# A transformer block in one launch, first gemm of its FFN: accumulating transfers that read the weights from HBM, a second quarter split by VectorE, a fourth quarter loaded once, and wide matmuls grouped by width

## The chip, the core and the metric

The kernel runs on one core of a Trainium2 chip. The metric is the device time of one execution in microseconds (us). Engines: TensorE (PE; PEld for its weight loads), VectorE (DVE), ScalarE (ACT), GpSimd (POOL, which here mostly issues transfers) and SyncE (SP, which issues the weight loads). PSUM is where matmuls leave their sums, SBUF where all other tiles lie, HBM the memory outside the core. Each engine works through its own list of instructions in order; an instruction that waits holds back all that stand behind it on that engine.

## The reference, cut to what matters

One block on 512 tokens of width 1024, all in fp32: a mixer with two attention branches, then a gated FFN, with a modulation by a condition vector. The change touches the FFN's first gemm alone (`w_ffn_in`, 1024 x 5632):

```python
h2 = modulate(rmsnorm(x, g_norm2[l]), shift2, scale2)
a, u = split(einsum('bsd,de->bse', h2, w_ffn_in[l]), 2)   # 2816 columns each
x = x + gate2[:, None, :] * einsum('bse,ed->bsd', silu(a) * u, w_ffn_out[l])
```

## The kernel before, in words

**Hi and lo.** TensorE multiplies in a rounded fp32 form, so every operand is split in two tiles: a rounded `hi`, and `lo`, which holds what the rounding lost. A product takes three matmuls: hi with hi, hi with lo and lo with hi. `high` (L846) makes hi by a ScalarE copy (L847). lo is made in one of two ways. `low` (L850) subtracts on VectorE, raw minus hi (L851). `low_dma` (L838) lets ScalarE write minus hi (L839) and then lets a transfer, issued by GpSimd, add the raw weight to it on the way (L840): an accumulating transfer, which reads the raw tile in SBUF. `split_dma` is `high` and then `low_dma`. The weights of the FFN's second gemm are split by ScalarE (L206) and VectorE (L208) after a load by L201.

**Blocks and products.** The 2816 columns of a and of u are cut into 11 blocks p = 0 to 10, 256 columns of a and 256 of u each. The weight of a block is a 2 x 2 of quarters (row half, column half), each 128 x 1024 elements or 512 KB: quarter (1,0) is called the second here and (1,1) the fourth. Instead of eight quarter products a block does seven, in the manner of Strassen and Winograd, with sums of quarters as weights:

```python
SUM = {5: ((0, 1), (0, 0)), 6: ((1, 1), 5), 4: ((1, 0), 6), 7: ((1, 1), (0, 1))}
```

So t5 = (0,1) - (0,0), t6 = (1,1) - t5, t4 = (1,0) - t6 and t7 = (1,1) - (0,1), on VectorE (L1222). Product 1 takes quarter (0,0), 2 takes (1,0), 3 takes (1,1), and 4 to 7 take t4 to t7. The activations' sums stand in SBUF as pairs, ah next to al (`v`, `qp`, `q`, `z` and so on by `act7`).

**Where weights come from.** `load_ff` (L1199) lets SyncE load a quarter. (0,0) and (1,0) go to a `raw` tile, of which there are 3 and which the second gemm's weights share; (0,1) and (1,1) go to an `araw` tile, of which there are 2. The fourth quarter is loaded twice in a block: into `araw` for the sums t6 and t7, and again into `raw` for product 3 (L1231). Products 1 and 2 get their lo by an accumulating transfer, product 3 and the sums by VectorE. `prepare` (L1225) does a weight's load, hi and lo; `prepare_item` (L1238) does it with the sums that are due.

**Two ways to multiply.** Blocks 0 and 1 use `product` (L1258), with matmuls 256 columns wide. Blocks from 2 on use `wide_product` (L1286): hi goes against ah and al side by side, 512 columns, and lo against ah, 256 columns, over 4 steps of the contraction into each of two PSUM banks: 16 matmuls in a product. `both_sums` (L1295) takes the two halves of a bank out, ScalarE by a copy (L1299) and VectorE by an add (L1300); `both_added` (L1303) does it by VectorE alone (L1308). Products 1, 6, 7 and 4 of a block go one after another into the same two banks, so 6 must be taken out before 7 starts.

**Order.** A list of work (L1418) puts a block's products as 1, 5, an item of the second gemm (`out`), 6, 2, 7, 3, 4, another `out`. Weights are prepared five items ahead (L1414). The first part, on products of blocks 0 and 1 and on the weights of block 2's products 1 and 2, is written out by hand (L1464 to L1598). Elsewhere a scheduler puts each engine's list in order; it is the tile framework's, and gives a load its place once the tile that it overwrites is due to be free.

Of the kernel before, what the change touches and what calls it, by code (L numbers as in the profile page):

```python
# [12 lines left out]
F32R = mybir.dt.float32r  # L13
I32 = mybir.dt.int32
AF = mybir.ActivationFunctionType
ALU = mybir.AluOpType
# [5 lines left out]
S = 512  # L22
# [70 lines left out]
WIDX = {e[0]: n for n, e in enumerate(PLAN)}  # L93
# [22 lines left out]
def kernel(  # L116
# [9 lines left out]
    nc = tc.nc  # L126
# [9 lines left out]
    def nm(s):  # L136
        uid[0] += 1
        return f"{s}_{uid[0]}"

    def ps():  # L140
        return pspool.tile([P, S], F32, tag="ps", bufs=BUFS["ps"], name=nm("ps"))
# [4 lines left out]
    def psz():  # L146
        return pspool.tile([P, S], F32, tag="z", bufs=BUFS["z"], name=nm("z"))
# [4 lines left out]
    def tmp():  # L152
        return apool.tile([P, S], F32, tag="t", bufs=BUFS["t"], name=nm("t"))
# [7 lines left out]
    def f(ap):  # L161
        return ap.bitcast(F32)
# [64 lines left out]
    def mm(o, lhs, rhs, start, stop):  # L227
        return nc.tensor.matmul(o, lhs, rhs, start=start, stop=stop, skip_group_check=True).ins  # L228
# [211 lines left out]
    with tc.manual_schedule(engines={nc.vector.engine, nc.scalar.engine, nc.tensor.engine}):  # L440

        nc.scalar.preload_act_table_set("natural_log_exp_and_others")
        c = sm[:, SM_C : SM_C + KT]
# [36 lines left out]
        for hv in HALVES:  # L480
            o = psz()[:, 0:256]
# [28 lines left out]
        for kt in range(KT):  # L510
# [8 lines left out]
            raw, hi, lo = wts[kt]  # L519
            ah, al = hs[kt][:, 0, :], hs[kt][:, 1, :]  # L520
# [303 lines left out]
    def quarter(tag):  # L824
        return pair(tag).rearrange("p a b -> p (a b)")

    def tiles(t):
        return t.rearrange("p (k c) -> p k c", k=4)

    def raw_quarter(tag):  # L830
        return apool.tile([P, 2 * S], F32, tag=tag, bufs=BUFS[tag], name=nm(tag))

    def wtile(tag):
        if tag in ("s", "h", "q", "v"):
            return quarter(tag)
        return wpool.tile([P, WCOLS], F32R, tag=tag, bufs=BUFS[tag], name=nm(tag))

    def low_dma(src, hi, lo):  # L838
        nc.scalar.activation(lo, f(hi), AF.Copy, scale=-1.0)  # L839
        nc.gpsimd.dma_start(f(lo), src, accum_op=ALU.add)  # L840
        return hi, lo

    def split_dma(src, hi, lo):
        return low_dma(src, high(src, hi), lo)

    def high(t, hi):  # L846
        nc.scalar.activation(hi, t, AF.Copy)  # L847
        return hi

    def low(t, hi, lo):  # L850
        nc.vector.tensor_sub(lo, t, f(hi))  # L851
        return hi, lo
# [242 lines left out]
    for h in range(17):  # L1095
        heads(h)
        p = h // 2 + 2
# [13 lines left out]
    for d in range(8):  # L1111
        o = ps()
        gemm(o, weight(("ps", d)), acts)
        r, t = tmp(), tmp()
# [60 lines left out]
    def high7(key, src, tags):  # L1175
        acts7[key] = two = [quarter(t) for t in tags]
        for n, t in enumerate(two):
            ins = nc.scalar.activation(
                parted(t)[:, :, 0, :], src[:, n * S : n * S + S].rearrange("p (k c) -> p k c", k=2), AF.Copy
            )  # L1180
        return ins.ins
# [9 lines left out]
    def act7(key, k):  # L1191
        t = acts7[key][k // 2]
        c = k % 2 * S
        return t[:, c : c + 256], t[:, c + 256 : c + S], t[:, c : c + S]

    ready = {}
    raws_of, sums_of = {}, {}

    def load_ff(p, half, c, tag):  # L1199
        if tag in ("h", "q"):  # L1200
            r = raw_quarter(tag)
            nc.sync.dma_start(r, wp[WIDX["ff", p, half, c]])
            return r
        r = wpool.tile([P, WCOLS], F32, tag=tag, bufs=BUFS[tag], name=nm(tag))
        nc.sync.dma_start(r, wp[WIDX["ff", p, half, c]])
        return r
# [3 lines left out]
    def load_raws(p, quarters):  # L1210
        raw = raws_of.setdefault(p, {})
        for q in quarters:
            if q not in raw:
                raw[q] = load_ff(p, *q, "araw" if q[1] else "raw")

    def sums(p, **tags):
        raw, t = raws_of[p], sums_of.setdefault(p, {})
        for key, tag in tags.items():
            n = int(key[1])
            a, b = SUM[n]  # L1220
            t[n] = raw_quarter(tag)
            ins = nc.vector.tensor_sub(t[n], raw[a], t[b] if b in t else raw[b])  # L1222
        return ins.ins

    def prepare(p, n, tags=None):  # L1225

        if n < 3:
            load_raws(p, [(n - 1, 0)])
            w = split_dma(raws_of[p][n - 1, 0], *(wtile(t) for t in tags or " sh"[n] * 2))
        elif n == 3:  # L1230
            raw = load_ff(p, 1, 1, "raw")  # L1231
            w = low(raw, high(raw, wtile("whi")), wtile("wlo"))
        else:
            t = sums_of[p][n]
            w = low(t, high(t, wtile("whi")), wtile("wlo"))
        ready[p, n] = w

    def prepare_item(it):  # L1238
# [3 lines left out]
        p, n = it  # L1242
        if p > 1 and n == (5 if p >= WIDE else 6):
            sums(p, t5="s", t6="s")
# [10 lines left out]
    SEVEN = {1: "A11", 2: "A12", 3: "S4", 4: "A22", 5: "S1", 6: "S2", 7: "S3"}  # L1255
# [30 lines left out]
    def wide_product(p, n, banks, first, last):  # L1286
        hi, lo = (tiles(t) for t in ready.pop((p, n)))
        for i, o in enumerate(banks):
            c = slice(i * P, (i + 1) * P)
            for k in range(4):  # L1290
                ah, _, both = act7(SEVEN[n], k)
                mm(o, hi[:, k, c], both, first and k == 0, False)
                mm(o[:, 256:S], lo[:, k, c], ah, False, last and k == 3)

    def both_sums(banks, t=None):  # L1295
        t = t or tmp()
# [14 lines left out]
    def run_wide(p, n):  # L1311
# [6 lines left out]
        elif n == 2:  # L1318
            d["y"] = [psz(), psz()]
        banks = d["v" if n in (3, 5) else "y" if n == 2 else "z"]  # L1320
        wide_product(p, n, banks, n in (1, 5, 2) or alone and n == 6, n in (2, 3, 4))
        added = (lambda b: both_added(d["p1"], b, tmp())) if alone else both_sums
        if n == 1:
# [20 lines left out]
    def store_act(p, *halves):  # L1344
# [3 lines left out]
            split(hi[:, :, hv], lo[:, :, hv], t.rearrange("p (a b) -> p a b", a=2))  # L1348
        ff_acts[chunk_of[p]] += [(hi[:, i, :], lo[:, i, :]) for i in range(2)]
        del part[p]  # L1350

    WIDE = 2

    def run_product(p, n):

        if p >= WIDE:
            return run_wide(p, n)
# [62 lines left out]
    for c, (p0, n) in enumerate(FF_CHUNKS):  # L1420
        for p in range(p0, p0 + n):
            wide = p >= 2
            for n_, m in enumerate((1, 6, 5, 2, 7, 3, 4) if p == 1 == WIDE else (1, 5, 6, 2, 7, 3, 4) if wide else (1, 6, 5, 7, 2, 4, 3)):
                if (p, m) not in FIRST:
# [13 lines left out]
    for d in range(4):  # L1438
        o = ps()
# [24 lines left out]
    with tc.manual_schedule(engines={nc.vector.engine, nc.scalar.engine, nc.tensor.engine}):  # L1464
# [55 lines left out]
        first = load_ff(1, 1, 0, "raw")  # L1520
        raws_of[1][1, 0] = first
        b_hi = high(first, wtile("whi"))
# [2 lines left out]
        )  # L1525
        d0["p1"] = tmp()
        nc.scalar.activation(d0["p1"], d0["x"], AF.Copy)
        ready[1, 2] = low_dma(first, b_hi, wtile("wlo"))
        k5 = high(t0[5], wtile("whi"))
        r1 = []  # L1530
        product(0, 2, d0["x2"], True, True, 4, lambda: r1.append(half_bcast(g1)))
# [10 lines left out]
        k1 = high(raws_of[2][0, 0], wtile("s"))  # L1542
# [12 lines left out]
        d0["z"], d0["v"], d0["w"] = psz(), psz(), psz()  # L1555
        product(0, 6, d0["z"], True, True, late="a")
        high7("S1", s1, ("qp", "q"))
        ready[2, 1] = low_dma(raws_of[2][0, 0], k1, wtile("s"))
        nc.vector.tensor_sub(s3, m00, s3)
        low7("S1", s1)  # L1560
        high7("S3", s3, "qq")
# [2 lines left out]
        d0["u2"] = tmp()  # L1564
        nc.vector.tensor_add(d0["u2"], d0["z"], d0["p1"])
        b22 = load_ff(0, 1, 1, "raw")
        ready[0, 3] = split_dma(b22, wtile("whi"), wtile("wlo"))
        high7("S4", s4, "qq")
        prepare(2, 2)
        load_raws(1, [(0, 1), (1, 1)])  # L1570
# [57 lines left out]
    for d in FULL:  # L1628
        o = ps()
# [158 lines left out]
```

## Time and profile before

| what | value |
|---|---|
| time, 3 runs | 1129.54 us median, 1128.47 to 1130.91 |
| time of the profiled execution | 1134.42 us |
| its span, first to last instruction | 1132.7 us |
| mean granted TensorE clock | 0.991 of full |
| VectorE, ScalarE, GpSimd busy | 868.0, 571.7, 49.9 us |
| HBM read, written | 146.35 MB, 16.78 MB |
| blocks 4 to 10 of the FFN's first gemm | 873 us to about 1100 us of the span |

A chain of waits lists start, length and what ran. A timeline row is start, length, engine, line, operation, tiles and shape; the bracket gives how long its engine had idled before it and what released it. A row of windows gives the window's ends and length, busy time (with instructions) of PE, PEld, DVE, ACT and POOL, then the granted clock, the share of the DMA engines' time, and GB/s. A row of waits is: who waited, for what, us in total, times, longest.

### The profile page before, as it was taken

The page shows a single profiled execution, that of the slowest core. Times are in us where ns is not written, and L with a number is a line of the kernel's source. Part 1 is how long each engine was busy: PE and PEld are TensorE (multiplying, and loading weights), DVE is VectorE, ACT ScalarE, POOL GpSimd, SP SyncE. Part 2 cuts the span into 40 slices and gives each one's busy share as a digit, 9 for nine tenths or more (in the row PEclk, how much of TensorE's full clock was granted, in tenths as well). Part 3 has the DMA queues.
Part 4 walks back from the last instruction along what each step waited for, and adds up shares of the span by engine and source line. Part 5 has one row for each costly group of instructions (what it writes and reads, how often), then busy time and mean ns, then how long its engine had stood idle before and what let it go on. Part 6 is the DMA issues. An engine that isn't in the chain of part 4 may idle for free.

```text
span 1132.7 us, 15139 instructions
## 1 busy us (share of the span) xinstructions
PE 1109.7 (98%) x5607; PEld 938.8 (83%) x5607; DVE 868.0 (77%) x1306; ACT 571.7 (50%) x935; POOL 49.9 (4%) x78
## 2 busy tenths in 40 slices
PE   8999999999999999999999999999999999999996
PEld 6888888887788888888888888899988788877886
DVE  7889856958977958387778757668999778868766
ACT  5445345434444645355656553449555545545543
POOL 0000000010020020000000000000000000000000
PEclk9999999999999999999999999999999999998998
DMA  9724432765775476866676569453547635555312
GB/s 353 284 71 149 140 120 81 221 134 196 240 166 196 157 156 231 220 195 186 182 205 160 161 194 320 157 146 81 165 128 193 201 96 161 168 149 152 90 56 76
DMA packets 63146, 190.86 MB, mean 169 GB/s; under 512 B 7776, under 2 KB 9824, under 8 KB 63072
## 3 DMA queue, kind: packets, MB, share of 16 engines
q1 hardware_dynamic: 55760, 171.02, 46.7%
q0 software_dynamic: 6768, 18.35, 9.5%
q8 instruction: 44, 0.72, 0.3%
q10 hardware_dynamic: 544, 0.52, 0.1%
q14 instruction: 30, 0.25, 0.1%
HBM read 146.35 MB, written 16.78 MB: 144 GB/s over the span
## 4 chain that ended last, share of the span: by engine, by line
PE 79%; DVE 10%; DMA 6%; issue 3%; ACT 2%; SPq 0%; DVEq 0%; ACTq 0%; POOLq 0%
PE ps L228 60%; PE z L228 11%; PE av L228 6%; DMA araw<-wada 2%; DMA raw<-wp 2%; DVE araw L256 1%; DVE wlo L851 1%; PE ps L636 1%; DVE s L870 1%; DVE wlo L208 1%; DMA s<-raw 1%; DMA sraw<-wada 1%; DVE t L758 0%; PE z L762 0%; DMA h<-raw 0%
## 5 line engine op out<-in xcount | busy, mean ns | idle before, releaser
L228 PE MATMUL ps<-h,whi 128*128 128x512 f32 (+1 forms) x1026 | 294.8, 372 | 0.0
L228 PEld LDWEIGHTS ps<-h,whi 128*128 128x128 f32 x1026 | 185.3, 189 | 32.1 <-ACT sm L410 0.2
L206 ACT ACTIVATE whi<-raw 128x1024 fp32r<-128x1024 f32 (+1 forms) x104 | 108.6, 1045 | 203.7 <-PE ps L228 160.4
L228 PE MATMUL ps<-h,wlo 128*128 128x512 f32 (+1 forms) x513 | 188.1, 370 | 0.0
L208 DVE TENSOR_TENSOR wlo<-raw,whi 128x1024 fp32r<-128x1024 f32 (+1 forms) x104 | 125.0, 1202 | 74.9 <-ACT whi L206 74.4
L228 PE MATMUL ps<-q,whi 128*128 128x512 f32 (+1 forms) x368 | 131.1, 402 | 5.8 <-DVE t L1300 5.7
L228 PEld LDWEIGHTS ps<-h,wlo 128*128 128x128 f32 x513 | 96.7, 188 | 16.6
L228 PE MATMUL ps<-s,whi 128*128 128x512 f32 x320 | 98.9, 390 | 0.3 <-DVE s L208 0.3
L228 PE MATMUL ps<-q,wlo 128*128 128x256 f32 (+1 forms) x328 | 97.4, 297 | 0.0
L228 PEld LDWEIGHTS ps<-q,whi 128*128 128x128 f32 x368 | 70.5, 193 | 24.3 <-DVE t L1300 8.1
L851 DVE TENSOR_TENSOR wlo<-s,whi 128x1024 fp32r<-128x1024 f32 x46 | 56.1, 1222 | 44.2 <-ACT whi L847 44.1
L847 ACT ACTIVATE whi<-s 128x1024 fp32r<-128x1024 f32 x47 | 49.6, 1058 | 51.4 <-PE ps L228 42.4
L228 PE MATMUL ps<-whi,h 128*128 128x512 f32 x222 | 71.6, 391 | 0.0
L228 PEld LDWEIGHTS ps<-s,whi 128*128 128x128 f32 x320 | 60.1, 188 | 13.2 <-DVE s L208 0.6
L228 PEld LDWEIGHTS ps<-q,wlo 128*128 128x128 f32 x328 | 63.9, 195 | 1.3
L228 PE MATMUL ps<-s,wlo 128*128 128x512 f32 x160 | 62.2, 389 | 0.0
L228 PEld LDWEIGHTS ps<-whi,h 128*128 128x128 f32 x222 | 41.7, 188 | 9.5 <-ACT t L991 0.6
L847 ACT ACTIVATE whi<-raw 128x1024 fp32r<-128x1024 f32 x28 | 29.7, 1059 | 34.1 <-PE ps L228 32.6
L256 DVE SCALAR_TENSOR_TENSOR araw<-araw,cact 128x1024 f32<-128x1024 f32 x32 | 39.1, 1228 | 8.4 <-DMA araw<-wada 8.3
L851 DVE TENSOR_TENSOR wlo<-raw,whi 128x1024 fp32r<-128x1024 f32 x26 | 31.8, 1223 | 16.7 <-ACT whi L847 16.7
L228 PE MATMUL ps<-wlo,h 128*128 128x512 f32 x111 | 43.2, 390 | 0.0
L1299 ACT ACTIVATE t<-ps 128x256 f32<-128x256 f32 x82 | 30.1, 372 | 23.1 <-PE ps L228 23.0
(349 smaller groups left out, 2242.5 us busy)
## 6 DMA issues: line engine op xcount, KB each, us to landing
raw<-wp SPq DMA_DIRECT2D x145, 512.0 KB, 4.0
araw<-wada SPq DMA_DIRECT2D x32, 512.0 KB, 4.0
araw<-wp SPq DMA_DIRECT2D x30, 512.0 KB, 4.6
s<-wp SPq DMA_DIRECT2D x24, 512.0 KB, 5.9
sraw<-wada SPq DMA_DIRECT2D x16, 512.0 KB, 8.0
q<-qp SPq DMA_DIRECT2D x32, 256.0 KB, 4.5
spill<-o POOLq DMA_DIRECT2D x24, 256.0 KB, 4.9
o<-xT SPq DMA_DIRECT2D x16, 256.0 KB, 4.4
```

What stands on the lines that cost most here:

```text
L206: nc.scalar.activation(dst_hi, src, AF.Copy, scale=scale)
L208: return (eng or nc.vector).tensor_sub(dst_lo, src, f(dst_hi))
L228: return nc.tensor.matmul(o, lhs, rhs, start=start, stop=stop, skip_group_check=True).ins
L256: nc.vector.scalar_tensor_tensor(raw, raw, 1.0, cact, op0=ALU.mult, op1=ALU.mult, accum_out=col)
L636: nc.tensor.transpose(at[bank][:, c : c + P], t[:, a + j * P : a + (j + 1) * P], ident)
L847: nc.scalar.activation(hi, t, AF.Copy)
L851: nc.vector.tensor_sub(lo, t, f(hi))
L870: nc.vector.tensor_tensor(dst[:, d], *((y, x) if swap else (x, y)), op=op)
L1299: nc.scalar.activation(c, o[:, 0:256], AF.Copy)
```

## The change

Four edits, all in the first gemm of the FFN:

- `low_dma`'s transfer takes the raw weight from HBM, where it was loaded from, not from the raw tile in SBUF. The raw tile is then read by the hi copy and the sums alone.
- For blocks from 2 on the second quarter's lo is made by `low` on VectorE, with no copy of minus hi and no transfer. In the part written by hand this is `prepare(2, 2)`.
- For blocks from 2 on product 3 uses the fourth quarter as it lies in `araw`; its second load is gone, and the `araw` tile is now read by t6, t7, and product 3's hi and lo.
- `wide_product` does the four 512-column matmuls of a bank first, and then its four 256-column ones.

```diff
     def low_dma(src, hi, lo):
         nc.scalar.activation(lo, f(hi), AF.Copy, scale=-1.0)
-        nc.gpsimd.dma_start(f(lo), src, accum_op=ALU.add)
+        nc.gpsimd.dma_start(lo, src.bitcast(F32R), accum_op=ALU.add)
...
+    WIDE, LOWD = 2, (2,)
...
         if n < 3:
             load_raws(p, [(n - 1, 0)])
-            w = split_dma(raws_of[p][n - 1, 0], *(wtile(t) for t in tags or " sh"[n] * 2))
+            hi, lo = (wtile(t) for t in tags or " sh"[n] * 2)
+            raw = raws_of[p][n - 1, 0]
+            w = (low(raw, high(raw, hi), lo) if p >= WIDE and n in LOWD else
+                 low_dma(wp[WIDX["ff", p, n - 1, 0]], high(raw, hi), lo))
         elif n == 3:
-            raw = load_ff(p, 1, 1, "raw")
+            raw = raws_of[p][1, 1] if p >= WIDE else load_ff(p, 1, 1, "raw")
             w = low(raw, high(raw, wtile("whi")), wtile("wlo"))
...
             for k in range(4):
-                ah, _, both = act7(SEVEN[n], k)
-                mm(o, hi[:, k, c], both, first and k == 0, False)
-                mm(o[:, 256:S], lo[:, k, c], ah, False, last and k == 3)
+                mm(o, hi[:, k, c], act7(SEVEN[n], k)[2], first and k == 0, False)
+            for k in range(4):
+                mm(o[:, 256:S], lo[:, k, c], act7(SEVEN[n], k)[0], False, last and k == 3)
...
-        ready[1, 2] = low_dma(first, b_hi, wtile("wlo"))
+        ready[1, 2] = low_dma(wp[WIDX["ff", 1, 1, 0]], b_hi, wtile("wlo"))
...
-        ready[2, 1] = low_dma(raws_of[2][0, 0], k1, wtile("s"))
+        ready[2, 1] = low_dma(wp[WIDX["ff", 2, 0, 0]], k1, wtile("s"))
...
-        ready[0, 3] = split_dma(b22, wtile("whi"), wtile("wlo"))
+        ready[0, 3] = low_dma(wp[WIDX["ff", 0, 1, 1]], high(b22, wtile("whi")), wtile("wlo"))
```

Lines of helpers move by one to four: L1299, L1300 and L1308 become L1303, L1304 and L1312, L1222 becomes L1223, L1205 becomes L1206.

TensorE's list before, at the start of product 1 of block 4 (`ps_7994` is the product's first PSUM bank, `v` the pair ah and al, `s_7829` the weight's hi and `s_7830` its lo):

```order
L228 MATMUL ps_7994<-v_6764,s_7829 128x512
L228 MATMUL ps_7994<-v_6764,s_7830 128x256
L228 MATMUL ps_7994<-v_6764,s_7829 128x512
L228 MATMUL ps_7994<-v_6764,s_7830 128x256
L228 MATMUL ps_7994<-v_6765,s_7829 128x512
L228 MATMUL ps_7994<-v_6765,s_7830 128x256
```

The same product after the change (`ps_7987` is its bank, `s_7823` hi and `s_7824` lo):

```order
L228 MATMUL ps_7987<-v_6764,s_7823 128x512 x2
L228 MATMUL ps_7987<-v_6765,s_7823 128x512 x2
L228 MATMUL ps_7987<-v_6764,s_7824 128x256 x2
L228 MATMUL ps_7987<-v_6765,s_7824 128x256 x2
```

The wide and the narrow matmuls of a bank no longer take turns; their number is the same.

VectorE's list before, in block 6 from the lo of its product 3 on (`raw_8573` is the fourth quarter's second load; `araw_8668`, `raw_8661` and `araw_8670` are block 7's (0,1), (0,0) and (1,1); the first L1222 is block 7's t5 and the second its t6; L1158 adds a result to the residual):

```order
L851 TENSOR_TENSOR wlo_8577<-raw_8573,whi_8575 128x1024
L1300 TENSOR_TENSOR t_8597<-t_8597,ps_8580 128x256
L1158 SCALAR_TENSOR_TENSOR o_6349<-z_8606,mod,o_6349 128x512
L1222 TENSOR_TENSOR s_8695<-araw_8668,raw_8661 128x1024
L1222 TENSOR_TENSOR s_8697<-araw_8670,s_8695 128x1024
L1158 SCALAR_TENSOR_TENSOR o_6351<-av_8620,mod,o_6351 128x512
L851 TENSOR_TENSOR wlo_8604<-h_8514,whi_8602 128x1024
L1300 TENSOR_TENSOR t_8656<-t_8656,ps_8550 128x256
L208 TENSOR_TENSOR wlo_8637<-raw_8634,whi_8636 128x1024
L1300 TENSOR_TENSOR t_8656<-t_8656,ps_8551 128x256
```

The same place after (`araw_8380` is block 6's fourth quarter, `araw_8655` block 7's, `t_8641` takes product 6 of block 6 out of its banks):

```order
L851 TENSOR_TENSOR wlo_8562<-araw_8380,whi_8560 128x1024
L1304 TENSOR_TENSOR t_8582<-t_8582,ps_8565 128x256
L1223 TENSOR_TENSOR s_8680<-araw_8653,raw_8646 128x1024
L1158 SCALAR_TENSOR_TENSOR o_6349<-z_8591,mod,o_6349 128x512
L1223 TENSOR_TENSOR s_8682<-araw_8655,s_8680 128x1024
L851 TENSOR_TENSOR wlo_8589<-h_8501,whi_8587 128x1024
L1158 SCALAR_TENSOR_TENSOR o_6351<-av_8605,mod,o_6351 128x512
L1304 TENSOR_TENSOR t_8641<-t_8641,ps_8537 128x256
L208 TENSOR_TENSOR wlo_8622<-raw_8619,whi_8621 128x1024
L1304 TENSOR_TENSOR t_8641<-t_8641,ps_8538 128x256
```

The order is nearly the same, but product 3's lo now reads the `araw` tile that block 7's fourth quarter will overwrite. In some blocks (7 is one) product 2's lo, a new L851, stands between the last two L1304.

SyncE's list before, from block 6's second load of its fourth quarter on:

```order
L1205 DMA raw_8573<-wp 128x1024
L201 DMA raw_8634<-wp 128x1024
L1205 DMA araw_8668<-wp 128x1024
L1205 DMA raw_8661<-wp 128x1024
L1205 DMA araw_8670<-wp 128x1024
L201 DMA raw_8725<-wp 128x1024
L1205 DMA raw_8785<-wp 128x1024
L1205 DMA raw_8851<-wp 128x1024
```

The same place after (`raw_8495` is block 6's second quarter):

```order
L1206 DMA raw_8495<-wp 128x1024
L201 DMA raw_8619<-wp 128x1024
L1206 DMA raw_8646<-wp 128x1024
L201 DMA raw_8710<-wp 128x1024
L1206 DMA araw_8653<-wp 128x1024
L1206 DMA araw_8655<-wp 128x1024
L1206 DMA raw_8770<-wp 128x1024
```

The loads `raw_8573` and `raw_8851` have no counterpart, and the two `araw` loads of block 7 stand behind one more load of the second gemm.

More of the change, by code (lines that the diff above doesn't have):

```diff
@@ L1350, in store_act @@
         del part[p]
-    WIDE = 2
     def run_product(p, n):
```

## The prediction

> **What bounds the kernel now.** I read the page first, for the engine that bounds; then the chain of waits, for the places where that engine's rhythm breaks; then the windows and the timeline there, and SyncE's waits. The page:
>
> ```profile
> span 1132.7 us, 15139 instructions
> ...
> PE 1109.7 (98%) x5607; PEld 938.8 (83%) x5607; DVE 868.0 (77%) x1306; ACT 571.7 (50%) x935; POOL 49.9 (4%) x78
> ```
>
> TensorE is busy for 98% of the span. So only three things count: matmul work, TensorE's few idle times, and its clock. In the chain the first product of a block shows as one piece of 32 matmuls. These are the starts of blocks 4, 5, 6, 9 and 10:
>
> ```profile
> 873.05 5.64 PE ps L228 x32
> 907.88 5.64 PE ps L228 x32
> 938.57 5.64 PE ps L228 x32
> 1037.88 5.64 PE ps L228 x32
> 1068.57 5.64 PE ps L228 x32
> ```
>
> Undisturbed, a block takes 938.57 - 907.88 = 30.69 us, as does 1068.57 - 1037.88. Block 4 took 34.83, so 4.14 too many. Blocks 6 to 8 took 99.31, against 3 x 30.69 = 92.07: 7.24 too many. Together 11.4 us. The windows on those two places, and on one undisturbed block:
>
> ```profile
> 873.00:904.00 31.00, 28.77 (x145) 24.13 (x144) 23.81 (x37) 15.41 (x23) 1.72 (x2) 0.94 0.63 176
> 1000.00:1038.00 38.00, 34.98 (x167) 29.13 (x166) 25.58 (x40) 17.92 (x27) 1.72 (x2) 0.91 0.53 152
> 1038.00:1068.60 30.60, 30.60 (x161) 26.10 (x160) 24.18 (x38) 15.09 (x24) 1.72 (x2) 1.00 0.33 87
> ```
>
> TensorE idles 31.00 - 28.77 = 2.2 us in the first and 3.0 in the second, and the clock costs 0.06 x 31 = 1.9 and 0.09 x 38 = 3.4: 4.1 and 6.4 of the 4.14 and 7.24. The first two rows below are the chain at the second place, the others its timeline:
>
> ```profile
> 1006.95 6.22 DMA s<-raw
> 1013.73 4.34 DMA raw<-wp
> ```
> ```profile
> 1013.31 0.33 SPq L201 DMA_DIRECT2D raw<-wp  x1
> 1018.18 1.06 ACT L847 ACTIVATE h<-raw 128x1024 fp32r<-128x1024 f32 x1 [5.22 <-DMA raw<-wp]
> 1019.54 0.42 DVE L1300 TENSOR_TENSOR t<-t,ps 128x256 f32<-128x256 f32 x1 [4.11 <-ACT t L1299]
> 1020.01 0.50 PE L228 MATMUL ps<-q,whi 128*128 128x512 f32 x1 [2.29 <-DVE t L1300]
> 1021.47 0.63 PE L228 MATMUL ps<-q,whi 128*128 128x512 f32 x1
> ```
>
> Read it downwards. An accumulating transfer lands at 1013.17, and until then holds the raw tile that it reads. Only then can SyncE issue the load of 1013.31, with the second quarter's load behind it at 1013.73. ScalarE, in order, has stood for 5.22 us at that quarter's hi; the PSUM copy L1299 stands behind it, VectorE's L1300 waits for the copy, and TensorE waits 2.29 us for the bank. Afterwards a wide matmul takes 0.63 us. At the first place the same chain; the first row is from SyncE's waits between 884 and 892 us:
>
> ```profile
> SPq L1205 <- DMA s<-raw: 6.4, 1, 6.4
> ```
> ```profile
> 894.23 1.06 ACT L847 ACTIVATE h<-raw 128x1024 fp32r<-128x1024 f32 x1 [6.01 <-DMA raw<-wp]
> 897.67 0.61 PE L228 MATMUL ps<-q,whi 128*128 128x512 f32 x1 [2.23 <-DVE t L1300]
> ```
>
> **The change, part by part.** *Transfers from HBM, second quarter on VectorE.* SyncE's waits for accumulating transfers between 840 and 1100 us:
>
> ```profile
> SPq L201 <- DMA s<-raw: 37.0, 3, 12.7
> SPq L1205 <- DMA s<-raw: 26.9, 4, 7.1
> SPq L201 <- DMA h<-raw: 22.2, 4, 9.2
> SPq L1205 <- DMA h<-raw: 11.0, 4, 7.2
> ```
>
> These 97 us go, because no transfer reads a raw tile any more. A raw tile is then free once ScalarE and VectorE have read it, and block 4's load, which came behind a wait of 6.4 us, could have been issued up to 6.4 us sooner. TensorE stood for 2.2 and 2.3 us, so both stalls vanish whole, and the lowered clock with them: **-11.4 us**. What is late next is the `araw` load, below. Bounds: 0, if the load is as late for another reason, and -11.4.
>
> Nine copies of minus hi and nine transfers go; nine subtractions come:
>
> ```profile
> L851 DVE TENSOR_TENSOR wlo<-raw,whi 128x1024 fp32r<-128x1024 f32 x26 | 31.8, 1223 | 16.7 <-ACT whi L847 16.7
> ```
>
> ScalarE, at half load, gets nine copies free: 0. By this row VectorE gets 9 x 1.22 more, one in a block: 24.18 + 1.22 = 25.4 of 30.7 us, 83%. TensorE hides it, unless it falls ahead of a PSUM add that TensorE waits for; that is priced below.
>
> The transfers that remain read the same 512 KB from HBM. The page of accumulating issues (min, median, max to landing) beside the plain loads:
>
> ```profile
> DMA to landing us min/median/max: 4.5/4.8/8.9
> ```
> ```profile
> raw<-wp SPq DMA_DIRECT2D x40, 512.0 KB, 3.6
> araw<-wp SPq DMA_DIRECT2D x14, 512.0 KB, 5.2
> ```
>
> Product 1's weight is issued a block ahead: a transfer from 1006.95 serves block 9, from 1037.88. That is 31 us of cover, and only a landing over 31 us would cost. I take 0.
>
> *Fourth quarter loaded once.* Nine loads of 512 KB go. In exchange block p+1's fourth quarter can't be loaded before block p's product 3 has its lo, and VectorE's t6 waits for it in order. Behind t6 stand t4's lo, a residual add, the lo of `out`, and the L1300 that takes product 6 out, which product 7 needs. Block 6's VectorE before:
>
> ```profile
> 945.22 1.23 DVE L851 TENSOR_TENSOR wlo<-raw,whi 128x1024 fp32r<-128x1024 f32 x1 [1.55 <-ACT whi L847]
> 948.91 1.23 DVE L1222 TENSOR_TENSOR s<-araw,s 128x1024 f32<-128x1024 f32 x1
> 950.05 0.74 DVE L1158 SCALAR_TENSOR_TENSOR o<-av,mod,o 128x512 f32<-128x512 f32 x1
> 953.50 1.23 DVE L208 TENSOR_TENSOR wlo<-raw,whi 128x1024 fp32r<-128x1024 f32 x1 [1.24 <-ACT whi L206]
> 954.64 0.41 DVE L1300 TENSOR_TENSOR t<-t,ps 128x256 f32<-128x256 f32 x1
> ```
> ```profile
> 949.67 2.71 PE ps L228 x15
> ```
>
> That lo ends at 946.45. The load lands 3.6 (raw's median) to 5.2 us (araw's) later: 950.1 to 951.7. With a residual add ahead of it t6 could start at 948.6, so VectorE waits 1.5 to 3.1 us. Then follow t6 1.2, t4's lo 1.2, residual 0.7, add 0.4, lo of `out` 1.2 and add 0.4, less 0.1 of overlap each: about 4.9 us, until 955.0 to 956.6. Product 6 ends at 952.38, product 2 takes 2.83, so product 7 starts at 955.2 and reaches its second bank 1.4 later, at 956.6. The wait is 0. In the blocks where product 2's lo stands in between too (+1.14), it is 0 to 1.1 us. For seven blocks that is 0 to 7.7 us; I take **+1.8**, nearer to 0, since VectorE had 30.60 - 24.18 = 6.4 us of slack in a block.
>
> *Opening.* `prepare(2, 2)` now puts a subtraction into VectorE's list, ahead of block 2's t5, in a stretch where one row follows on the other without a pause. The lo that is needed soonest after it:
>
> ```profile
> 802.68 1.22 DVE L851 TENSOR_TENSOR wlo<-s,whi 128x1024 fp32r<-128x1024 f32 x1
> ```
>
> What follows is 1.2 us later, and up to 1.1 more (one hi copy, as L847 above) if its hi isn't ready. The lo of 802.68 is used a few us later. 0 to +2.3, I take **+0.5**: TensorE's next products have weights ready.
>
> *Wide matmuls grouped.* The chain has pieces of one width each and mixed ones:
>
> ```profile
> 913.52 2.74 PE z L228 x12
> 797.07 2.88 PE z L228 x24
> 918.98 2.81 PE ps L228 x16
> 921.79 2.83 PE z L228 x16
> ```
>
> Twelve wide ones: 2.74/12 = 0.2283 us each. Twenty-four narrow ones: 0.120 each. A grouped product is 8 x 0.2283 + 8 x 0.120 = 2.786 against 2.81 to 2.83: 0.024 to 0.044 less. Block 2 has 5 wide products left, 8 blocks have 7: 61 x 0.034 = **-2.1** (-1.5 to -2.7; 0 if a change of width costs nothing).
>
> A weight load takes 0.195 us by the next row, longer than a narrow matmul's 0.120:
>
> ```profile
> L228 PEld LDWEIGHTS ps<-q,wlo 128*128 128x128 f32 x328 | 63.9, 195 | 1.3
> ```
>
> So a load runs beside matmuls of its own rows. The Trainium skill, TensorE: Matmul & The Clock Gate, section "The mechanism", has it that a weight load overlaps matmuls in flight only where row groups differ; here all use all rows, so load and matmul would add up in any order and this term would be 0. The trace disagrees: 0.120 us is less than the 0.195 of one load.
>
> **Sum.** 1134.4 - 11.4 - 2.1 + 0.5 + 1.8 = 1123.2 us for an execution like the profiled one. That one lies 4.9 over the median of the runs. If the 4.9 belongs to profiling, the timed runs fall to 1118.3; if the timed runs merely had less of those stalls, they land at 1123.2. I take the middle, **1121.0**.
>
> **Rivals.** *The gain is eaten, or was never there.* Either the second quarter's load stays late for another reason, or the `araw` wait takes 5 to 8 us. With grouping alone: 1129.5 - 2.1 = 1127.4; with grouping and VectorE's other costs 1127 to 1131. For it: SyncE's list is in order, and the `araw` load now stands in it waiting for VectorE, ahead of the next second quarter. Against it: both stalls lead back to an accumulating transfer by name. Chance 0.16.
>
> *Slower: the fourth quarter holds TensorE up in every block.* Place: t6, behind an `araw` load that lands over 6.5 us after its issue, where 5.2 is the median. VectorE then runs 2.3 us or more late at product 6's add, TensorE idles as at 897.67, and each stall costs what block 4's did, 4.14 us with its clock. From the third on, the 8.5 us forecast are gone; with five of seven blocks 1121 + 5 x 4.1 = 1141.5, with eight 1154. For it: two loads issued together shared the DMA engines. Against it: a block's DMA share is 0.33 where nothing is late, and eleven loads and transfers become nine or ten. Chance 0.13.
>
> Here a rule would change the price. In the trace, 2.23 us of idling were followed by matmuls of 0.61 to 0.63 us and a window clock of 0.94. The Trainium skill, TensorE: Matmul & The Clock Gate, section "HAM oscillation — how this bites in real kernels", lets the clock fall for idle gaps over about 3.4 us; by it five stalls of 2.3 us would cost 11.5 and end near 1132.5, still slower. The trace disagrees: 2.2 us was enough.
>
> *The forecast* has the rest, 0.71, own range 1115 to 1126.
>
> **How the numbers follow.** The forecast's range takes the unknown terms at both ends: 1118.3 less 2.3 for a late wait that never comes and 0.6 for grouping gives 1115; 1123.2 with 2.5 more of waits gives 1126. To hold 8 in 10 it reaches into the first rival, up to 1129, and one down, 1114. About 0.2% (2.3 us) is what a measurement of this kernel can tell from no change. Faster by more, under 1127.2: the forecast and a little of the first rival, 0.73. Within: 0.13, the rest of that rival. Slower, above 1131.8: 0.14, the second rival and a sliver of the first.
>
> **What would show it.** Right: blocks 4 to 9 all near 30.2 to 30.7 us apart; SyncE's waits name no accumulating transfer; the granted clock is 1.00 in every block; a wide product takes 2.78 to 2.79 us; VectorE waits 1.5 to 3.1 us at L1223 for `araw<-wp`, and TensorE's waits for L1304 stay under 1 us a block. Wrong: L847 on a second quarter still idles over 5 us for `raw<-wp`; or TensorE's waits for L1304 recur in most blocks with a clock under 0.95; or a product still takes 2.82 us.

## The result, and the profile after

The changed kernel takes 1119.9 us (median of 4 runs, 1119.4 to 1120.14) against 1130.17 for the kernel before on the same chip: a ratio of 0.9911, 95% interval 0.9893 to 0.9928. Forecast were 1121.0 us, a ratio of 0.992. The page of the changed kernel:

```profile
span 1118.0 us, 15104 instructions
...
PE 1101.4 (99%) x5607; PEld 934.7 (84%) x5607; DVE 876.9 (78%) x1315; ACT 562.4 (50%) x926; POOL 42.2 (4%) x69
```

The chain of waits of the changed kernel, starts of blocks 4, 5, 9 and 10, with the piece that follows block 9's first two products, twelve matmuls of the second gemm:

```profile
870.53 5.58 PE ps L228 x32
901.09 5.59 PE ps L228 x32
1023.36 5.58 PE ps L228 x32
1028.94 2.77 PE z L228 x12
1053.93 5.59 PE ps L228 x32
```

Block 4 takes 30.56 us, block 9 takes 30.57, and blocks 5 to 8 take 122.27, four times 30.57: the 4.14 and the 7.24 us are gone. TensorE's waits between 700 and 1110 us, and VectorE's for the fourth quarter's and its neighbour's loads between 830 and 1095:

```profile
PE ps L228 <- ACT t L1595: 1.2, 1, 1.2
```
```profile
DVE s L1223 <- DMA araw<-wp: 8.4, 5, 3.2
```

VectorE waits for `araw` as forecast, five times; TensorE never feels it. TensorE's one wait of more than 0.3 us is in the part written by hand. Its start can be set apart from what the change doesn't touch: shortly before that part the chain has one piece of 15 matmuls, and 54 matmuls later on stand in one piece too. Before, and then after:

```profile
773.06 1.90 PE ps L228 x15
802.83 7.15 PE z L228 x54
```
```profile
769.44 1.90 PE ps L228 x15
800.61 7.15 PE z L228 x54
```

29.77 us between them before, 31.17 after: the hand-written part lost 1.40 us. And the profiled execution of before came to this point 3.6 us later than that of after, with the same instructions up to there but for the source of three transfers; in the twelve runs below, with either source, the point lies between 767.7 and 772.4. So 3.6 of the 14.7 us between the two spans can't be put down to the change. From here on **tail** is the time from the start of that piece to the span's end: 1132.7 - 773.06 = 359.6 before, 1118.0 - 769.44 = 348.6 after. The change is worth 11.1 us by the tails: 11.4 of stalls and 1.1 of shorter blocks, less 1.4 in the hand-written part. One profiled execution stands behind each tail, and that of before is a long one: the timed executions of before in this record took 1124.0 to 1134.5 us at granted clocks of 0.991 to 0.998, and the profiled one had 0.991. The stalls differ from one execution to the next, and how they are made up in a median one is not shown.

### The profile page after: what moved, and what is told of

Its sections match the earlier page's. It is cut to its first block, busy times and chain, and to the rows that moved or that the text cites. A ratio compares the mean times of both kernels' runs of the same rounds, so it can differ in the third digit from the quotient of the medians.

```text
span 1118.0 us, 15104 instructions
## 1 busy us (share of the span) xinstructions
PE 1101.4 (99%) x5607; PEld 934.7 (84%) x5607; DVE 876.9 (78%) x1315; ACT 562.4 (50%) x926; POOL 42.2 (4%) x69
## 4 chain that ended last, share of the span: by engine, by line
PE 82%; DVE 11%; DMA 3%; ACT 2%; issue 1%; SPq 0%; DVEq 0%; ACTq 0%
PE ps L228 61%; PE z L228 12%; PE av L228 7%; DMA araw<-wada 3%; DVE araw L256 2%; DVE wlo L851 1%; PE ps L636 1%; DVE s L870 1%; DVE wlo L208 1%; DMA sraw<-wada 1%; DVE t L758 0%; ACT whi L847 0%; PE z L762 0%; DVE s L209 0%; DVE t L1033 0%
## 5 line engine op out<-in xcount | busy, mean ns | idle before, releaser
L206 ACT ACTIVATE whi<-raw 128x1024 fp32r<-128x1024 f32 (+1 forms) x104 | 108.6, 1044 | 195.7 <-PE ps L228 154.8
L228 PE MATMUL ps<-q,whi 128*128 128x512 f32 (+1 forms) x368 | 103.8, 388 | 0.0
L851 DVE TENSOR_TENSOR wlo<-s,whi 128x1024 fp32r<-128x1024 f32 x46 | 56.1, 1222 | 42.3 <-ACT whi L847 42.3
L228 PEld LDWEIGHTS ps<-q,whi 128*128 128x128 f32 x368 | 65.2, 188 | 10.9
L228 PE MATMUL ps<-q,wlo 128*128 128x256 f32 (+1 forms) x328 | 63.4, 291 | 0.0
L228 PEld LDWEIGHTS ps<-q,wlo 128*128 128x128 f32 x328 | 51.7, 189 | 5.7
L1303 ACT ACTIVATE t<-ps 128x256 f32<-128x256 f32 x82 | 30.7, 374 | 32.8 <-PE ps L228 32.7
L228 PE MATMUL ps<-whi,q 128*128 128x512 f32 x128 | 40.7, 389 | 0.0
L847 ACT ACTIVATE whi<-h 128x1024 fp32r<-128x1024 f32 x20 | 21.2, 1060 | 37.9 <-PE av L228 29.1
```

The lines of the kernel that those rows point to most:

```text
L206: nc.scalar.activation(dst_hi, src, AF.Copy, scale=scale)
L1303: nc.scalar.activation(c, o[:, 0:256], AF.Copy)
```

## The experiments

The first four rows were measured together on one chip, the next four on another, the last four on the first again.

| kernel | what it is | median, us (range, runs) | ratio to before (95%) | tail |
|---|---|---|---|---|
| hbm_only | before + transfers from HBM | 1129.33 (1126.03 to 1135.3, 12) | 1.0002 (0.9982 to 1.0021) | 356.9 |
| second_only | before + second quarter on VectorE | 1124.97 (1121.82 to 1127.1, 9) | 0.9948 (0.993 to 0.9966) | 353.0 |
| fourth_only | before + fourth quarter loaded once | 1121.11 (1119.85 to 1122.11, 6) | 0.9919 (0.9898 to 0.994) | 350.2 |
| group_only | before + grouping | 1124.33 (1121.45 to 1125.15, 6) | 0.9943 (0.992 to 0.9965) | 354.5 |
| sbuf_rest | after - transfers from HBM | 1120.58 (1118.12 to 1122.24, 6) | 0.9935 (0.9911 to 0.996) | 348.9 |
| fourth_twice | after - fourth loaded once | 1120.89 (1119.45 to 1124.99, 8) | 0.9945 (0.9924 to 0.9966) | 348.8 |
| open_transfer | after, block 2's second quarter by transfer | 1118.93 (1117.74 to 1120.17, 6) | 0.9921 (0.9896 to 0.9947) | 347.2 |
| fourth_group | before + fourth once + grouping | 1122.14 (1121.12 to 1122.7, 8) | 0.995 (0.9932 to 0.9969) | 351.1 |
| after_again | after | 1118.91 (1117.69 to 1121.35, 6) | 0.991 (0.9892 to 0.9927) | 348.6 |
| no_second | after - second quarter on VectorE | 1127.53 (1125.56 to 1131.27, 12) | 0.9986 (0.9972 to 1.0) | 355.1 |
| no_group | after - grouping | 1121.99 (1120.68 to 1123.96, 6) | 0.9936 (0.9921 to 0.9951) | 350.7 |
| extra3 | after + 3.4 us of VectorE a block | 1124.14 (1123.9 to 1124.28, 5) | 0.9953 (0.9939 to 0.9966) | 353.3 |

### Each edit alone

**hbm_only**

```diff
-        nc.gpsimd.dma_start(f(lo), src, accum_op=ALU.add)
+        nc.gpsimd.dma_start(lo, src.bitcast(F32R), accum_op=ALU.add)
...
-            w = split_dma(raws_of[p][n - 1, 0], *(wtile(t) for t in tags or " sh"[n] * 2))
+            hi, lo = (wtile(t) for t in tags or " sh"[n] * 2)
+            w = low_dma(wp[WIDX["ff", p, n - 1, 0]], high(raws_of[p][n - 1, 0], hi), lo)
```

and the three calls written by hand as in the change.

> The kernel before with the transfers' source alone changed (HBM for the raw tile); second quarter by transfer, fourth quarter loaded twice, matmuls interleaved. Theory (the accumulating transfers held the raw tiles): both stalls go, 11.4 us less, ratio about 0.990, blocks 30.69 us apart throughout, granted clock 1.00 in all of them. Rival (five loads a block through three raw tiles are too many, whatever reads them): the second quarter's load stays late, gain under 3 us, ratio over 0.997.

No gain in the median (by the interval 2.0 us at most), and the prediction's theory fell with it. SyncE no longer waits for a transfer at all, and TensorE still stalls, here in blocks 3 and 7. The chain of hbm_only at its second stall (two pieces), then its timeline:

```profile
973.14 0.31 DVE wlo L851
...
974.40 6.54 DMA raw<-wp
```
```profile
981.05 1.06 ACT L847 ACTIVATE h<-raw 128x1024 fp32r<-128x1024 f32 x1 [5.88 <-DMA raw<-wp]
982.88 0.79 PE L228 MATMUL ps<-q,whi 128*128 128x512 f32 x1 [2.94 <-DVE t L1301]
```
```profile
SPq L201 <- DVE s L1222: 42.9, 5, 12.5
```

The second quarter's load lands as late as before, and its hi holds up ScalarE and the PSUM copy as before. Two things took the place of the transfer's hold. The first is the next holder: the load's raw tile is freed at 974.37 by product 3's lo (L851 from 973.14, 1.23 us), which reads the fourth quarter's second copy, and a load ahead of it in SyncE's list (L201) had waited for t5, which reads block p+1's first quarter. The trace of before had this holder in it. Product 3's lo in block 8, which reads the tile that the load of 1013.73 took, ended at 1012.65, 0.5 us before the transfer landed:

```profile
1011.43 1.22 DVE L851 TENSOR_TENSOR wlo<-raw,whi 128x1024 fp32r<-128x1024 f32 x1
```

The second is the transfer itself. It no longer comes before the load but runs beside it; hbm_only, the issue of that transfer:

```profile
972.70 0.87 POOL L840 DMA_DIRECT2D s<-wp  x1 [9.57 <-ACT s L839]
```

That transfer landed 7.4 us later, at 980.1. Beside it the load took 6.54 us to land, where the load of 1013.73 took 4.34. Counted from the moment at which TensorE stopped (1017.72 before, 979.94 here), the load was issued 1.55 us sooner than before and took 2.20 longer, so it landed 0.65 later, and TensorE's wait is 2.94 in place of 2.29 us. Three raw tiles had four users at that moment. Taking away the last of them to let go made the load 1.55 us earlier, not 6.4 or 12.7 as long as the waits that it had ended, and the slower landing took more than that away. What the removal would gain if the load landed as fast as before, no run shows.

The edit makes loads slower throughout. Median times to landing between 840 and 1100 us, hbm_only (its counterparts of before stand in the prediction: 3.6 and 5.2 us for the loads, 4.5, 4.8, 8.9 for accumulating transfers):

```profile
raw<-wp SPq DMA_DIRECT2D x39, 512.0 KB, 4.2
araw<-wp SPq DMA_DIRECT2D x14, 512.0 KB, 5.8
h<-wp POOLq DMA_DIRECT2D x8, 512.0 KB, 7.1
```

**second_only**: in `prepare`, with the transfers from SBUF,

```diff
+            w = (low(raw, high(raw, hi), lo) if p >= WIDE and n in LOWD else
+                 low_dma(raw, high(raw, hi), lo))
```

> The kernel before with the second quarter split by VectorE for blocks from 2 on, and nothing else; product 1's transfers still read the raw tile. Theory (holds): both stalls of before led back to product 1's transfer, so at least one of them stays; the opening loses 1.4 us as in the changed kernel: 1126 to 1132 us, ratio 0.997 to 1.001. Rival (too many loads): no load is gone, 1130 to 1132 us. Should it come near 1120 us, the second quarter's own transfers were the hold that mattered.

Faster than expected: 0.9948, and its tail holds the hand-written part's 1.4 us as well. What was left of a stall came in two short waits, and the clock stayed whole (the last row is the window on them):

```profile
1015.10 0.51 PE L228 MATMUL ps<-q,whi 128*128 128x512 f32 x1 [1.07 <-DVE t L1304]
1017.70 0.51 PE L228 MATMUL ps<-q,whi 128*128 128x512 f32 x1 [0.92 <-DVE t L1304]
```
```profile
1005.00:1025.00 20.00, 18.01 (x96) 15.01 (x96) 15.53 (x23) 7.18 (x11) 0.00 (x0) 1.00 0.45 138
```

So product 1's transfer, to which the prediction put the stalls down, may go on holding raw tiles: with product 2's hold ended sooner, most of what the stalls cost is gone. The tail is still 4.4 us over that of after, of which the pitch of grouping has 1.1.

**fourth_only**

```diff
-            raw = load_ff(p, 1, 1, "raw")
+            raw = raws_of[p][1, 1] if p >= WIDE else load_ff(p, 1, 1, "raw")
```

> The kernel before with the fourth quarter loaded once for blocks from 2 on, and nothing else; all transfers still read raw tiles. Theory (holds): the transfers still hold raw tiles, but four loads a block instead of five go through them, so the stalls shrink by a part at most: 1122 to 1130 us, and SyncE still waits over 50 us for accumulating transfers. Rival (too many loads): both stalls go, 1119 us, ratio 0.990.

The rival was right: 0.9919, about as much as the whole change (by the tails 9.4 of its 11.1 us). TensorE's waits from 700 us on, and one of SyncE's:

```profile
PE ps L228 <- DVE t L1301: 0.9, 2, 0.6
```
```profile
SPq L1206 <- DMA s<-raw: 38.0, 5, 10.1
```

SyncE still waits for transfers, 78 us in all; with four loads a block through the raw tiles that delays almost nothing that TensorE needs.

**group_only**: the change's last edit on the kernel before.

> The kernel before with the wide matmuls grouped by width, and nothing else. From the changed kernel's blocks (30.57 us apart against 30.69): 61 products of 0.018 us, 1.1 us less, ratio 0.999; both stalls stay (TensorE waits for the PSUM add over 2 us twice). The prediction's 2.1 us would give 0.998. Rival (the shorter blocks of the changed kernel come from something other than the grouping): blocks stay 30.69 us apart, ratio 1.000.

Far more than its pitch: 0.9943. TensorE still waits 5.7 us in all, as before, in six waits of at most 1.4 us. TensorE at the place of before's first stall, and the window on it:

```profile
891.92 1.20 PE L228 MATMUL ps<-q,whi 128*128 128x512 f32 x4 [1.08 <-DVE t L1300]
894.53 1.20 PE L228 MATMUL ps<-q,whi 128*128 128x512 f32 x4 [0.94 <-DVE t L1300]
```
```profile
870.00:901.00 31.00, 28.98 (x150) 24.49 (x149) 24.97 (x39) 16.55 (x25) 1.72 (x2) 1.00 0.65 190
```

2.0 us of idling, nearly as much as the 2.2 of before, but in two parts, and the clock stays at 1.00: the 1.9 and 3.4 us that the lowered clock took are saved (between 1005 and 1025 us, on the wait of 1.4, the clock is 1.00 too). The edit moved more than matmuls. ScalarE's list in block 4, before and here (L1331 is the Silu):

```
L839 ACTIVATE h_8232<-h_8231 128x1024          L839 ACTIVATE h_8232<-h_8231 128x1024
L1331 ACTIVATE t_8012<-t_8012 128x512          L1299 ACTIVATE t_8163<-ps_7994 128x256
L1299 ACTIVATE t_8163<-ps_7994 128x256         L1331 ACTIVATE t_8012<-t_8012 128x512
```

The scheduler put the PSUM copy, for which TensorE waits, ahead of a Silu of 0.6 us. That explains about half of the 1.15 us by which the first part is shorter than before's 2.23. The rest is the second quarter's load, which landed 20.5 us after the block's first matmul (868.40 to 888.88) and not 21.2 (872.89 to 894.12); why it came sooner was not traced.

### One edit undone

**sbuf_rest**: the transfer edit taken back everywhere.

> The changed kernel with all its accumulating transfers reading the raw tile in SBUF again. Theory now: with four loads a block the hold costs nothing, 1119 to 1121 us, ratio 0.991, while SyncE waits for accumulating transfers again. The prediction's theory (holds): both stalls led back to product 1's transfers, so at least one returns, 1123 us or more.

As the new theory had it: no stall in the wide blocks, while SyncE waits for transfers again (`SPq L1206 <- DMA s<-raw`, 24.2 us in three waits). In the changed kernel, with one transfer a block, the source is worth nothing that these runs can tell. With two a block, reading from HBM costs time (fourth_group, below).

**fourth_twice**

```diff
-            raw = raws_of[p][1, 1] if p >= WIDE else load_ff(p, 1, 1, "raw")
+            raw = load_ff(p, 1, 1, "raw")
```

> The changed kernel with the fourth quarter's second load put back (into a raw tile, for product 3); transfers from HBM, second quarter on VectorE and grouping as in the changed kernel. Theory now (three raw tiles are too few for five loads a block; the transfer's hold was only the one that came last, and with it gone the load waits for product 3's lo): TensorE waits for the PSUM add again, at least one stall of 1 us or more after 830 us, 1122 to 1127 us, ratio 0.994 to 0.998. Rival (any two of the edits are enough): no stall, 1119 to 1121 us.

Mostly the rival: no stall in the profile, six of eight runs between 1119.45 and 1121.84. Two took 1124.7 and 1125.0, which fits a stall now and then, but no trace of one of these was taken. So the second load is not by itself the cause either.

**no_second**: `LOWD = ()`.

> The changed kernel with every second quarter split by a transfer from HBM again, the opening's too. Theory now (fewer loads, or shorter holds, are each enough where transfers don't read raw tiles): no stall after 830 us, and the opening's 1.4 us come back: 1118.3 to 1119.3 us. Rival (the second quarter's split by VectorE is needed): a stall over 1 us, 1121 us or more.

A miss, and the run that tells most: without VectorE's split the other three edits lose nearly all of the gain. The stalls are of the kind that the prediction had as its slower rival. VectorE in block 7, with the chain's load of the fourth quarter, and TensorE:

```profile
974.03 1.23 DVE L1223 TENSOR_TENSOR s<-araw,raw 128x1024 f32<-128x1024 f32 x1 [4.09 <-DMA araw<-wp]
975.17 1.22 DVE L851 TENSOR_TENSOR wlo<-araw,whi 128x1024 fp32r<-128x1024 f32 x1
981.40 1.22 DVE L1223 TENSOR_TENSOR s<-araw,s 128x1024 f32<-128x1024 f32 x1 [3.37 <-DMA araw<-wp]
984.15 2.07 PE L228 MATMUL ps<-q,whi 128*128 128x512 f32 x4 [3.08 <-DVE t L1304]
```
```profile
966.94 6.99 DMA araw<-wp
...
976.41 4.89 DMA araw<-wp
```
```profile
963.00:994.00 31.00, 27.92 (x144) 23.86 (x143) 23.16 (x35) 15.07 (x23) 2.58 (x3) 0.94 0.63 169
```

t5 waits 4.09 us for a load that took 6.99. Product 3's lo stands behind t5, and holds the `araw` tile until 976.39. Only then comes the fourth quarter's load; t6 waits 3.37 us for it, product 6's add stands behind t6, and TensorE waits 3.08 and loses its clock. In the changed kernel's list, product 3's lo stands ahead of t5 (VectorE's list after the change, shown above for block 6; block 7 has it so too: 968.48 against 970.44); here the scheduler put t5 first. The order alone is not the whole of it: fourth_group, below, has the same order and faster loads, and loses less.

**no_group**: the interleaved loop in the changed kernel.

> The changed kernel with its wide matmuls interleaved again. With no stall to shorten, grouping is worth its pitch alone: 1.1 us (61 products of 0.018), so 1120.5 to 1121.7 us, blocks 30.69 us apart, and no stall after 830 us. The prediction's 2.1 us would give 1122. Rival (the grouped order also keeps stalls away): a stall over 1 us returns, 1123 us or more.

3.1 us more than after_again on the same chip, 2.1 by the tails; the pitch explains 1.1. Two of six runs took 1123.9. Another 0.3 us is a wait of TensorE near 836 us, for a hi by ScalarE (L206), that after_again doesn't have. No wait of TensorE over 1.2 us is in the profile, so the rest stays open.

### Other runs

**open_transfer**: `if p > WIDE and n in LOWD` in place of `p >= WIDE`.

> The changed kernel with the second quarter of block 2 alone, in the part written by hand, split by a transfer again (from HBM). If the subtraction there is what held VectorE, ScalarE's PSUM copy and so TensorE up for 1.2 to 1.4 us, that wait is gone: 1118.5 us, 1.2 to 1.4 us under the changed kernel, and TensorE's wait for ScalarE's PSUM copy near 795 us is 0. Rival (TensorE would have waited there anyway): 1119.9 us.

The wait is gone, and the tail is 347.2, 1.4 less. By the time it is the fastest of its four, 1.6 us under sbuf_rest; against the changed kernel, measured on another chip, the ratios to before (0.9921 and 0.991) don't tell the two apart. What it removes, in the changed kernel's timeline:

```profile
788.84 1.23 DVE L851 TENSOR_TENSOR h<-h,h 128x1024 fp32r<-128x1024 f32 x1 [1.11 <-ACT h L847]
794.18 0.63 ACT L1583 ACTIVATE t<-t 128x512 f32<-128x512 f32 x1 [2.94 <-DVE t L1581]
796.83 0.58 ACT L1595 ACTIVATE t<-ps 128x512 f32<-128x512 f32 x1
797.47 3.14 PE L228 MATMUL ps<-v,h 128*128 128x256 f32 x24 [1.16 <-ACT t L1595]
```

The new lo waits 1.11 us for its hi and delays all behind it. ScalarE then stands 2.94 us at a Silu that needs one of VectorE's adds, and behind that Silu stands the PSUM copy for which TensorE waits.

**fourth_group**: two edits of the four on the kernel before.

> The kernel before with two of the four edits, the fourth quarter loaded once and the matmuls grouped; transfers from SBUF, second quarter by a transfer. Theory now: the fourth quarter takes the stalls away, grouping gives 1.1 us, and the opening's loss isn't there: 1118 to 1119.5 us, at or under the changed kernel. Rival (the other two edits are needed as well): 1121 us or more.

Worse than expected, with four waits of TensorE of 0.2 to 1.4 us, and no better than the fourth quarter alone. VectorE's list has t5 ahead of product 3's lo in block 7 as in no_second. It differs from that kernel in the transfers' source alone, and its tail is 4.0 us shorter; the ratios, each to before on its own chip, lie apart too (0.9932 to 0.9969 here, 0.9972 to 1.0 there). So with two transfers a block it costs time to read from HBM. Medians to landing here are 3.7 us (raw), 4.3 (araw) and 5.7 (accumulating, to `h`); in no_second 4.0, 5.1 and 7.1.

**after_again**: no edit.

> The changed kernel as it is, beside the two that undo one edit each: 1119.4 to 1120.6 us, no stall of TensorE after 830 us, as in its first profile. If stalls come now and then in it as well, some executions are 3 to 5 us longer.

Within 0.1% of the first result; no stall in the wide blocks.

**extra3**

```diff
-            ins = nc.vector.tensor_sub(t[n], raw[a], t[b] if b in t else raw[b])
+            for _ in range(4 if n == 6 and p > WIDE else 1):
+                ins = nc.vector.tensor_sub(t[n], raw[a], t[b] if b in t else raw[b])
```

> The changed kernel with t6 computed four times over instead of once in blocks 3 to 10, 3.4 us more of VectorE a block (28.8 of 30.6 us); what is computed stays the same. This tries the prediction's slower rival: a late VectorE ahead of product 6's PSUM add. In the changed kernel that add is done 1.2 us before TensorE needs the bank. If all 3.4 us fall ahead of it, TensorE waits 2.2 us a block in 8 blocks: 1137 us with the clock at 1.00, 1153 us if each wait costs block 4's 4.14. If the scheduler spreads the additional work into VectorE's slack: 1119 to 1124 us.

From block 4 on the scheduler spread the work; near block 3 it did not. A window in block 6, one near block 3, and TensorE at its only stall of note:

```profile
932.00:963.00 31.00, 31.00 (x164) 26.53 (x163) 29.91 (x44) 15.91 (x25) 0.85 (x1) 1.00 0.42 119
830.00:845.00 15.00, 12.06 (x56) 9.92 (x55) 15.00 (x24) 3.19 (x3) 0.00 (x0) 0.89 0.31 107
```
```profile
840.43 1.85 PE L228 MATMUL ps<-q,whi 128*128 128x512 f32 x4 [2.94 <-DVE t L1313]
```

In block 6 VectorE is busy for 29.91 of 31 us and TensorE doesn't wait; blocks stay 30.55 us apart. The 4.7 us more in the tail are one wait of 2.94 near block 3 with its clock (0.89 between 830 and 845 us). VectorE there, up to the adds for which TensorE waited:

```profile
833.62 1.22 DVE L1224 TENSOR_TENSOR s<-araw,s 128x1024 f32<-128x1024 f32 x1
834.76 1.22 DVE L851 TENSOR_TENSOR wlo<-s,whi 128x1024 fp32r<-128x1024 f32 x1
835.90 1.22 DVE L1224 TENSOR_TENSOR s<-araw,s 128x1024 f32<-128x1024 f32 x1
837.03 0.41 DVE L1313 TENSOR_TENSOR t<-t,ps 128x256 f32<-128x256 f32 x1
837.36 1.21 DVE L1224 TENSOR_TENSOR s<-araw,s 128x1024 f32<-128x1024 f32 x1
838.50 0.41 DVE L1313 TENSOR_TENSOR t<-t,ps 128x256 f32<-128x256 f32 x1
838.83 1.22 DVE L1224 TENSOR_TENSOR s<-araw,s 128x1024 f32<-128x1024 f32 x1
839.97 0.74 DVE L1313 TENSOR_TENSOR t<-t,ps 128x256 f32<-128x256 f32 x2
```

It waits for nothing: the four t6 stand between the adds that take a bank out, and VectorE is busy for all of the 15 us. In the changed kernel, too, it is busy for 34.30 of the 35 us from 825 to 860. So the amount of VectorE's work is hidden where it has slack, and holds TensorE up where it has none; the stalls of no_second, in which VectorE waits for loads, are another kind.

## Why the forecast held, and which of its steps did not

**Both stalls gone, -11.4 us: right in size, wrong in cause.** Two stalls of 4.14 and 7.24 us went. The step that failed is "These 97 us go ... so both stalls vanish whole": it took the wait that ended last for the cause, and the whole length of that wait for what its removal would gain. hbm_only removed all of these waits and gained nothing that its runs can tell; fourth_only kept 78 us of them and lost the stalls; sbuf_rest put 24 us of them back and lost nothing. The prediction asked what is late next and named the `araw` load. In the kernel with that edit alone it was product 3's lo on the next raw tile, by which the second quarter's load came 1.55 us sooner, and the load's landing beside the transfer, 2.20 us slower. What the runs show in place of the cause: five loads a block through three raw tiles, two of them held by transfers, left little room for a late one. Each of three edits takes a large part of the loss away on its own (by the tails 9.4, 6.6 and 5.1 us of the whole change's 11.1): one load less (0.9919), a hold that ends sooner (0.9948), or grouping, with which the waits stay but are too short to lower the clock (0.9943). Their gains don't add, because there were only 11.4 us of stalls to remove. Had the edits been priced one by one, the forecast would have gone to the one that gives nothing alone. That the sum came out right is in part luck: its terms add up to -11.2 us, what the tails show to -11.1, with 1.0 too much gain for grouping and 0.9 too little loss in the opening against 1.8 for a wait that cost nothing.

**Second quarter on VectorE, +1.22 us a block at 0: right, and more.** In the changed kernel TensorE waits for VectorE nowhere after 830 us, and extra3 hides 3.4 us more a block from block 4 on, though not near block 3. That the edit decides whether the fourth quarter's is harmless (no_second, +8.6 us over after_again) was not foreseen: it comes about by the order that the scheduler makes, with product 3's lo ahead of t5, and by loads that are slower beside two transfers from HBM a block. How much each of the two weighs stays open.

**`araw` wait, +1.8 us (0 to 7.7): 0.** VectorE waited up to 3.2 us, as walked through (1.5 to 3.1), and product 6's add still came in time. The mechanism is real: in no_second it took TensorE 3.08 us and a clock of 0.94. The count beside that rival, eleven loads and transfers that become nine or ten, is not in the rows: with five loads into raw tiles, two into `araw` tiles and two transfers a block has nine, and after the change seven.

**Opening, +0.5 us (0 to 2.3): 1.4.** Inside the range, at another victim: the prediction looked at the next lo on VectorE, and the delay reached TensorE by ScalarE, over a Silu and the PSUM copy behind it.

**Grouping, -2.1 us (-1.5 to -2.7): -1.1 by the blocks.** A block lost 0.12 us, 0.018 a product. The first two products take 5.58 in place of 5.64 us, 0.03 each as worked out, but the second gemm's twelve matmuls take 2.77 after a grouped product (row at 1028.94) where they took 2.74 before, twice a block. That makes 0.15 a block; the last 0.03 were not traced. The other way in which grouping alone helped, waits that stay short and leave the clock whole, was not in the working at all.

**Profile and median.** The 4.9 us between the profiled execution and the median were split down the middle. By the starts of the hand-written part 3.6 of them lie before it (773.06 against 769.44), outside these stalls; the other 1.3 stay open. With the 3.6 taken off, 1134.4 - 3.6 - 11.4 - 1.1 + 1.4 = 1119.7, against 1119.9 and 1118.9 measured.

**The clock.** The row against the Trainium skill's rule of about 3.4 us (TensorE: Matmul & The Clock Gate, section "HAM oscillation — how this bites in real kernels") stands, with more cases. Waits of TensorE of 2.94 (hbm_only, extra3) and 3.08 us (no_second) also lowered the clock, all of them shorter than 3.4; one of 2.44 did not.

## What to carry to other kernels

A wait's releaser is only the last of several holders: before crediting a gain to its removal, list what else holds the same buffers at that moment and when each lets go, what will run beside what no longer waits, and what stands in the in-order lists behind it. Several edits that each relieve one queue don't add up, so try them alone and undone one at a time. Where a scheduler makes the lists, compare the order on every engine, those too that the edit doesn't name: here grouping, an edit to TensorE's list only, moved PSUM copies on ScalarE too, and alone it gained 5.1 us by the tails where the matmuls that it was about give 1.1.

## What the runs showed of the hardware

**Short waits cost themselves, long ones the clock, and the border is not sharp.** Two waits of TensorE around 1 us, 2.6 us apart (group_only), left the clock at 1.00. Waits of 2.23 and 2.29 us lowered it (before), and one of 2.44 did not; hbm_only, TensorE and the window on it:

```profile
865.10 0.50 PE L228 MATMUL ps<-q,whi 128*128 128x512 f32 x1 [2.44 <-DVE t L1301]
```
```profile
860.00:871.00 11.00, 8.55 (x42) 6.84 (x41) 7.93 (x13) 7.04 (x10) 0.85 (x1) 1.00 0.44 112
```

**With two a block, accumulating transfers that read HBM land later, and loads beside them too.** Medians went from 4.6 to 7.1 us (to `h`) and from 3.6 to 4.2 for raw loads (before against hbm_only), and where the source alone differs from 5.7 to 7.1 and from 3.7 to 4.0 (fourth_group against no_second). With one a block the runs don't agree: 6.0 us from SBUF (sbuf_rest) against 6.9 (after) and 5.8 (fourth_twice) from HBM, and 3.5 for raw loads in all three.
